# An attention and gated-linear-attention block on one core: the attention units' instructions in the order of the source, their weights loaded from ScalarE's queue, and a unit's first two weight groups taken tile by tile

## The chip, the cores and the metric

The kernel runs on one core of a Trainium2 chip. A core has five engines with a queue of instructions each: TensorE (PE in the profile, with its weight loads as PEld), VectorE (DVE), ScalarE (ACT), GpSimd (POOL) and SyncE (SP), which here only issues transfers. The metric is the device time of one execution in microseconds.

## The reference

One encoder block on a sequence of 512 tokens of width 2048, all float32:

```python
mod = silu(c) @ w_cond + b_cond                     # shift, scale, gate
h = rms_norm(x) * (1 + scale) + shift
proj = h @ w_in                                     # 2048 x 7200
aq, ak, av, ag, gq, gk, gv, gg, lr_f, lr_b = split(proj)
# 16 heads x 64: three dilated windows, merged by their softmax denominators, shared bias by distance
a_out = dilated_attention(aq, ak, av, rel_bias) * silu(ag)
# 4 heads, dk 128, dv 256: gated linear attention, forward and backward, decay from lr_f and lr_b
g_out = rms_norm(gla_fwd + gla_bwd) * gain * silu(gg)
y = concat(a_out, g_out) @ w_out
out = rms_norm(x + gate * y) * final_gain
```

## The kernel before

Every large product is made of three matmuls (`three`): each operand is split into a high part, rounded to the type that TensorE takes in one pass, and a low part, the remainder, and high x high, high x low and low x high are summed. A weight group is 128 x 1024 numbers (0.5 MB). `fetch` loads it into one of four `raw` buffers, `split_hi` makes the high part on ScalarE and `split_lo` the low part on DVE (a split); there are three buffers for high parts and three for low parts.

After a start that computes shift and scale, the values and the first queries and keys, the work is a row of **units**: qk2, qk4, qk6, gk, gv0, gv1, ag0, ag1, gg0, gg1, o0 to o3. A unit multiplies eight weight groups with the 512 tokens into four accumulators (tiles) of 128 x 512 in PSUM. For each group it goes over the four tiles, with two steps (ticks) of three matmuls for each, so a unit has 64 ticks and 192 projection matmuls. While it runs a group it splits the next and fetches those behind. There are five PSUM buffers for accumulators, tagged `pj`, and three for everything else, tagged `pa`. In the names of the rows, ps_qk_0 is the first accumulator of such a unit, qk40h the high part of unit qk4's group 0, and qk41l the low part of its group 1.

Between the ticks a unit does **side work**, a list of pairs (place in the unit from 0 to 1, step). In qk2, qk4, qk6 and gk it is the attention of four heads each, 16 tiles of scores of 128 queries x 512 keys. One tile's steps:

- `score`: two matmuls; DVE adds the bias tile `g` of the head and finds the row's minimum; ScalarE takes the exponential with the row sums; DVE takes the reciprocal and GpSimd scales the rows
- `turn`: four transposes on TensorE; ScalarE copies the result (high part), DVE subtracts it (low part)
- `values`, for two tiles at once: eight matmuls; ScalarE copies one half and DVE adds it to the other

A place of 1 or more moves a step into the next unit. When a unit of queries and keys ends, `qk_evict` takes its four accumulators apart, two for each pair of heads: for each accumulator ScalarE copies one half for one head, DVE the remainder, and again for the other head, and SyncE copies halves between partitions. These are the queries and keys of the next unit's attention.

`sum_work` is a list of 48 weighted sums on DVE over 0.5 MB each, loaded into the same `raw` buffers: 16 for a bias of the values and 32 for the gate. `SUMS_IN` says how many of them each unit takes as side work.

The **order of the work** is set in two ways. TensorE's instructions stand in the order of the source. On the other engines the first part has an order that a planner computes; from `qk_evict` on, a list scheduler places each instruction by priority and by when its operands are expected, and side work has a raised priority (`urgent`). SyncE issues nearly all transfers.

Of the kernel before, what the change touches and what calls it, by code (L numbers as in the profile page):

```python
# [72 lines left out]
ATT_AT = (0.17, 0.8, 0.04, 0.05, 0.05)  # L73
# [4 lines left out]
SUMS_IN = {"qk6": 4, "gk": 4, "gv0": 9, "gv1": 2, "ag0": 7, "ag1": 9, "gg0": 9}  # L78
# [55 lines left out]
def block_kernel(ctx: ExitStack, tc: tile.TileContext, a: dict):  # L134
# [421 lines left out]
    def attention(pairs):  # L556

        tiles = [(2 * p + j, i) for p in pairs for j in range(2) for i in range(4)]
        gt, pt, pr_ = {}, {}, {}
        heads = [2 * p + j for p in pairs for j in range(2)]  # L560

        def g_load(h):
            g = gp.tile([P, 896], F32, tag="g", name=f"g{h}")
            nc.sync.dma_start(g, bass.AP(grow.tensor, grow.offset + h * 1024, [[1, P], [1, 896]]))
            gt[h] = g

        def score(h, i):
            def go():
                if h % 8 == 0 and i == 0:
                    cat[h // 8] = B8(f"cat{h // 8}", [4, 512])  # L570
# [12 lines left out]
                act(t, t, AF.Exp, bias=st[:, 0:1], scale=-1.0, accum_out=st[:, 1:2])  # L583
                nc.vector.reciprocal(st[:, 2:3], st[:, 1:2])  # L584
# [4 lines left out]
        def turn(h, i):  # L589
            def go():  # L590
# [7 lines left out]
                hi = pt[h, half][:, 0, :, P * ii:P * ii + P]  # L598
                lo = pt[h, half][:, 1, :, P * ii:P * ii + P]
# [4 lines left out]

        def values(h, half):
            def go():
                t = pt.pop((h, half))
# [25 lines left out]
        at[0] -= move0  # L633
        at[1] -= move1
        at[-1] += move_last
        return list(zip(at, items))
# [206 lines left out]
    def unit(name, natural, side=(), rhs=None, lr=None, tiles=range(4)):  # L843
# [287 lines left out]
```

## Time and profile before

| | |
|---|---|
| runs | 958.15, 958.9 and 960.98 us, median 958.9 |
| the profiled execution | 959.9 us, its span 957.9 us |
| busy: PE, PEld, DVE, ACT, POOL | 939.7, 777.1, 605.3, 431.5, 81.1 us |
| granted clock of TensorE | 0.997 of full, as a mean |
| read from memory | 154.51 MB, 166 GB/s over the span |
| qk2, qk4, qk6, gk | 191.9 to 257.3, to 323.7, to 390.3, to 457.5 us |
| gv0 | 457.5 to 510.4 us |

Matmuls are pipelined, so a matmul's row lasts longer (0.39 us) than the distance to the next one (0.23 us); the chain of waits shows the distance. A row of the timeline gives its start, its length, the engine and line, what is written and read, and in brackets the idle time before it and what ended that. Buffer numbers are left out of names in the profile.

### The profile page before, as it was taken

What the parts mean: (1) busy time and instruction counts of PE and PEld (TensorE: products, weight loads), DVE (VectorE), ACT (ScalarE), POOL (GpSimd) and SP (SyncE); (2) the same over time, 40 slices, a digit from 0 to 9 for tenths busy, and PEclk for the clock granted to TensorE, in tenths of its full rate; (3) what the DMA queues carried; (4) which work ended last, traced back from release to release, by engine and by line L of the source; (5) the groups of instructions that cost most, each with busy time, mean ns of one, the idle gap of its engine ahead of it and who ended that gap; (6) DMA issues with size and microseconds to landing.
All of it is one profiled execution on the core that took longest, in us unless ns stands there. A gap on an engine that the chain in (4) does not pass through costs nothing.

```text
span 957.9 us, 11999 instructions
## 1 busy us (share of the span) xinstructions
PE 939.7 (98%) x4464; PEld 777.1 (81%) x4464; DVE 605.3 (63%) x900; ACT 431.5 (45%) x719; POOL 81.1 (8%) x100
## 2 busy tenths in 40 slices
PE   8999999999999999999999999999999999999996
PEld 5888788888888888888778888888887888888884
DVE  7988899675756676766435656675964352546421
ACT  5443533565655655655215544543834152233222
POOL 0000000012122022122000000000010000202120
PEclk9999999999999999999999999999999999999998
DMA  9999687443333463533454244354555464244013
GB/s 330 413 411 365 229 296 275 150 131 105 112 103 105 144 200 108 173 127 103 150 176 146 86 132 154 132 176 154 173 195 183 132 221 154 92 151 152 23 55 121
DMA packets 45180, 163.76 MB, mean 171 GB/s; under 512 B 5730, under 2 KB 6018, under 8 KB 40386
## 3 DMA queue, kind: packets, MB, share of 16 engines
q1 hardware_dynamic: 44946, 162.68, 49.9%
q8 instruction: 35, 0.57, 0.2%
q10 hardware_dynamic: 176, 0.33, 0.1%
q14 instruction: 23, 0.18, 0.1%
HBM read 154.51 MB, written 4.28 MB: 166 GB/s over the span
## 4 chain that ended last, share of the span: by engine, by line
PE 84%; DMA 6%; DVE 5%; issue 3%; ACT 1%; SPq 0%; POOL 0%; ACTq 0%; DVEq 0%; POOLq 0%
PE ps_o L170 6%; PE ps_o L169 6%; PE ps_o L171 6%; DMA rawg<-in_wg 6%; PE ps_qk L170 5%; PE ps_qk L169 5%; PE ps_qk L171 5%; PE o L611 3%; PE sta L169 3%; PE sta L170 3%; PE sta L171 3%; PE stb L171 3%; PE stb L169 3%; PE stb L170 3%; PE ps_gv L171 3%; PE ps_gv L170 3%
## 5 line engine op out<-in xcount | busy, mean ns | idle before, releaser
L585 POOL TENSOR_SCALAR p<-p,st 128x512 f32<-128x512 f32 x64 | 45.5, 711 | 406.6 <-DVE st L584 357.9
L244 DVE CUSTOM_DVE_ANT_0 cb<-cb,sb,c_bcond 128x2048 f32<-128x2048 f32 (+1 forms) x32 | 73.4, 2294 | 0.0
L583 ACT ACTIVATE p<-p,st 128x512 f32<-128x512 f32 x64 | 46.1, 721 | 56.8 <-DVE st L580 56.3
L602 DVE TENSOR_TENSOR pt<-t,pt 128x512 fp32r<-128x512 f32 x64 | 44.0, 689 | 16.2 <-ACT pt L601 15.8
L580 DVE CUSTOM_DVE_ANT_0 p<-s,g 128x512 f32<-128x512 f32 x64 | 43.6, 687 | 14.8 <-PE s L577 14.5
L601 ACT ACTIVATE pt<-t 128x512 fp32r<-128x512 f32 x64 | 37.8, 592 | 10.2 <-PE t L597 9.2
L244 DVE CUSTOM_DVE_ANT_0 rawg<-rawg,sb,gate 128x1024 f32<-128x1024 f32 x16 | 20.5, 1283 | 29.6 <-DMA rawg<-in_wg 29.6
L611 PEld LDWEIGHTS o<-pt,vv 128*128 128x128 f32 x256 | 34.7, 188 | 5.0 <-DVE pt L602 2.2
L597 PEld LDWEIGHTS t<-c_ident,p 128*128 128x128 f32 x256 | 31.8, 140 | 8.5
L597 PE MATMUL t<-c_ident,p 128*128 128x128 f32 x256 | 38.3, 272 | 0.0
L611 PE MATMUL o<-pt,vv 128*128 128x256 f32 x256 | 36.6, 283 | 0.9 <-DVE pt L602 0.8
L244 DVE CUSTOM_DVE_ANT_0 rawg<-rawg,sb,c_bcond 128x1024 f32<-128x1024 f32 x16 | 20.5, 1283 | 26.3 <-DMA rawg<-in_wg 26.3
L1014 POOL TENSOR_TENSOR x<-x,fgain 128x512 f32<-128x512 f32 x12 | 20.3, 1696 | 185.3 <-ACT ysq L1012 185.3
L1012 ACT ACTIVATE ysq<-x 128x512 f32<-128x512 f32 x16 | 10.1, 632 | 47.2 <-DVE x L1010 47.2
L767 POOL TENSOR_SCALAR dc<-st,sc 128x256 f32<-128x256 f32 x16 | 10.4, 652 | 245.5 <-DVE st L764 240.6
L1009 DVE TENSOR_TENSOR y<-ps_o,sb 128x512 f32<-128x512 f32 x16 | 10.9, 684 | 25.9 <-PE ps_o L171 25.9
L584 DVE RECIPROCAL st<-st 128x1 f32<-128x1 f32 x64 | 10.3, 162 | 24.9 <-ACT p L583 24.9
L576 PE MATMUL s<-ks,qs 128*128 128x512 f32 x64 | 25.1, 391 | 0.0
L577 PE MATMUL s<-kl,qs 128*128 128x512 f32 x64 | 25.0, 391 | 0.0
L774 ACT ACTIVATE sq<-st,sc 128x256 f32<-128x256 f32 x24 | 12.2, 509 | 26.8 <-DVE st L769 14.3
L1010 DVE TENSOR_TENSOR x<-y,x 128x512 f32<-128x512 f32 x16 | 18.0, 1125 | 0.3
L614 ACT ACTIVATE oh<-o 64x256 f32<-64x256 f32 x32 | 12.2, 382 | 13.0 <-PE o L611 12.2
(1275 smaller groups left out, 2916.7 us busy)
## 6 DMA issues: line engine op xcount, KB each, us to landing
cb<-in_wm SPq DMA_DIRECT2D x31, 1024.0 KB, 7.9
rawg<-in_wg SPq DMA_DIRECT2D x32, 512.0 KB, 3.4
raw_o<-in_w_o SPq DMA_DIRECT2D x32, 512.0 KB, 3.4
raw_qk<-in_w_qk SPq DMA_DIRECT2D x24, 512.0 KB, 3.4
rawb<-in_w_sb SPq DMA_DIRECT2D x16, 512.0 KB, 4.8
rawv<-in_wv SPq DMA_DIRECT2D x16, 512.0 KB, 3.8
raw_gv<-in_w_gv SPq DMA_DIRECT2D x16, 512.0 KB, 3.5
raw_ag<-in_w_ag SPq DMA_DIRECT2D x16, 512.0 KB, 3.3
```

The source lines that it names most:

```text
L169: mm(ps, lh, rh, start=first, stop=False)
L170: mm(ps, ll, rh, start=False, stop=False)
L171: mm(ps, lh, rl, start=False, stop=last)
L244: nc.vector.tensor_tensor_reduce(out=w, in0=w, in1=with_, op0=ALU.mult, op1=ALU.add, scale=1.0, scalar=init, accum_out=dst)
L576: mm(ps, qs[:, q], ks, start=True, stop=False)
L580: nc.vector.tensor_tensor_reduce(out=t, in0=ps, in1=gt[h][:, P * i:P * i + 512], op0=ALU.add, op1=ALU.min, scale=1.0, scalar=3e38, accum_o ...
L583: act(t, t, AF.Exp, bias=st[:, 0:1], scale=-1.0, accum_out=st[:, 1:2])
L585: nc.gpsimd.tensor_scalar(t, t, st[:, 2:3], 1.0, op0=ALU.mult, op1=ALU.mult)
L597: nc.tensor.transpose(pk[:, kt * P:kt * P + P], t[:, kt * P:kt * P + P], ident)
L601: act(hi, src, AF.Copy)
L602: tt(lo, src, hi.bitcast(F32), op=ALU.subtract)
L611: mm(po[:, :256], vv[h // 4][:, kt, h % 4, :], t[:, w, kt, :], start=kt == 0 and w == 0, stop=kt == 3 and w == 1)
```

## The change

It does five things. (1) From the first `qk_evict` to the end of gv0's matmuls, `tc.manual_schedule(engines=PLANNED)` gives DVE, ScalarE, GpSimd and SyncE the order of the source too. (2) The places of the attention's steps are new: a tile's score stands at 0.12 + 0.057 x of the unit (x from 0 to 15), its scaling 0.75 steps later, its turn 1.8 and its values 2.9 steps later; the last tiles' steps fall into the next unit. Scaling is a step of its own. (3) The weight groups of qk2, qk4, qk6 and gk and the bias tiles `g` are loaded from ScalarE's queue. (4) In these four units the first two groups are one step: each tile is taken through both before the next tile begins, and both have to be split. (5) The sums leave qk6 and gk; gv0 gets 12 (9 before), gv1 5 (2), ag0 8 (7), and gg1 the remaining 5 (4). The low-rank gate weights `lrs` are loaded and split in gk instead of behind it. The diff also brings another way of turning tiles, through memory (`turn`, `leave`, `back` and two more), which an empty `BY_DVE` leaves unused; it is left out here.

```diff
-ATT_AT = (0.17, 0.8, 0.04, 0.05, 0.05)
+ATT_AT = (0.12, 0.057)
+BY_DVE = ()
...
-SUMS_IN = {"qk6": 4, "gk": 4, "gv0": 9, "gv1": 2, "ag0": 7, "ag1": 9, "gg0": 9}
+SUMS_IN = {"gv0": 12, "gv1": 5, "ag0": 8, "ag1": 9, "gg0": 9}
...
             raws[i] = RAW(f"raw_{u}{g}", [2, 512])
-            nc.sync.dma_start(raws[i], a["w_" + u][g])
+            queue = nc.scalar if u[:2] in ("qk", "gk") else nc.sync
+            queue.dma_start(raws[i], a["w_" + u][g])
...
-            nc.sync.dma_start(g, bass.AP(grow.tensor, grow.offset + h * 1024, [[1, P], [1, 896]]))
+            nc.scalar.dma_start(g, bass.AP(grow.tensor, grow.offset + h * 1024, [[1, P], [1, 896]]))
...
                 act(t, t, AF.Exp, bias=st[:, 0:1], scale=-1.0, accum_out=st[:, 1:2])
+                pr_[h, i] = t, st
+            return go
+
+        def scale(h, i):
+
+            def go():
+                t, st = pr_.pop((h, i))
                 nc.vector.reciprocal(st[:, 2:3], st[:, 1:2])
                 nc.gpsimd.tensor_scalar(t, t, st[:, 2:3], 1.0, op0=ALU.mult, op1=ALU.mult)
                 pr_[h, i] = t
             return go
...
-        for x in range(n + 4):
-            if x < n:
-                items.append(score(*tiles[x]))
-            if 2 <= x <= n + 1:
-                items.append(turn(*tiles[x - 2]))
-            if 3 <= x <= n + 2 and tiles[x - 3][1] % 2 == 1:
-                items.append(values(tiles[x - 3][0], tiles[x - 3][1] // 2))
+        for x in range(n):
+            h, i = tiles[x]
+            items.append((x, score(h, i)))
+            items.append((x + 0.75, scale(h, i)))
...
+                items.append((x + 1.8, pe_turn(h, i)))
+                if ii:
+                    items.append((x + 2.9, values(h, half)))
+        items.sort(key=lambda v: v[0])
         g_load(heads[0])
-        start, span, move0, move1, move_last = ATT_AT
-        at = [start + (q + 0.5) / len(items) * span for q in range(len(items))]
...
+        start, step = ATT_AT
+        return [(start + step * x, go) for x, go in items]
...
-        for q in range(KT // 2):
-            g = gorder[q] if name == "o3" else q
-            i0 = gi[name, g]
+        order_ = gorder if name == "o3" else list(range(KT // 2))
+
+        steps = [order_[:2]] if name[:2] in ("qk", "gk") else [order_[:1], order_[1:2]]
+        for step in steps + [[g] for g in order_[2:]]:
             todo = []
             if 0 in tiles:
-                todo = list(range(gi[name, gorder[0] if name == "o3" else 0], upto[name, g] + 1))
+                todo = list(range(gi[name, order_[0]], upto[name, step[-1]] + 1))
                 for i in todo:
                     split_hi(i)
                 for ahead in (1, 2):
-                    fetch(upto[name, g] + ahead)
-            if i0 not in low:
-                split_lo(i0)
-            hi, lo = wts[i0]
+                    fetch(upto[name, step[-1]] + ahead)
+            for g in step:
+                split_lo(gi[name, g])
             for n, i in enumerate(tiles):
-                for kk in range(2):
...
+                for g in step:
+                    hi, lo = wts[gi[name, g]]
+                    for kk in range(2):
...
-    for p in range(2):
-        qk_evict(p, psb["b", 4 + 2 * p], psb["b", 5 + 2 * p])
-    for n, p in (("qk2", 0), ("qk4", 2), ("qk6", 4)):
-        ps = unit(n, False, attention((p, p + 1)) + ([(0.05, shift_row)] + some_sums(n) if p == 4 else []))
...
+    with tc.manual_schedule(engines=PLANNED):
+        for p in range(2):
+            qk_evict(p, psb["b", 4 + 2 * p], psb["b", 5 + 2 * p])
+        for n, p in (("qk2", 0), ("qk4", 2), ("qk6", 4)):
+            ps = unit(n, False, attention((p, p + 1)) + ([(0.6, shift_row)] if p == 4 else []))
+            for q in range(2):
+                qk_evict(p + 2 + q, ps[2 * q], ps[2 * q + 1])
...
+        ps = unit("gk", False, attention((6, 7)) + [(0.7, lr_load), (0.85, lambda: lr_part(0)), (0.9, lambda: lr_part(1))])
...
+        ps = unit("gv0", True, some_sums("gv0"), lr=lr_tick)
```

How this moves instructions shows in the order in which they stand on an engine. First ScalarE at the boundary from qk2 to qk4, before (p is a tile's exponential, pt the copy of a turn, oh that of a values step, qs and ks the evicted halves of queries and keys):

```order
L313 ACTIVATE qk41h<-raw_qk_1961 128x1024
L583 ACTIVATE p_2036,st_2037<-p_2036,st_2037 128x512
L601 ACTIVATE pt_2004<-t_2050 128x4x128
L539 ACTIVATE qs_2106<-ps_qk_0_1509 64x512
L601 ACTIVATE pt_2061<-t_2062 128x4x128
L539 ACTIVATE qs_2109<-ps_qk_0_1509 64x512
L614 ACTIVATE oh_2081<-o_2072 64x256
L548 ACTIVATE ks_2112<-ps_qk_1_1510 64x512
L601 ACTIVATE pt_2061<-t_2090 128x4x128
L548 ACTIVATE ks_2118<-ps_qk_1_1510 64x512
L539 ACTIVATE qs_2124<-ps_qk_2_1511 64x512
L313 ACTIVATE qk42h<-raw_qk_2045 128x1024
```

And the same place on ScalarE after the change:

```order
L586 ACTIVATE p_2072,st_2073<-p_2072,st_2073 128x512
L544 ACTIVATE qs_2079<-ps_qk_0_1511 64x512
L544 ACTIVATE qs_2082<-ps_qk_0_1511 64x512
L553 ACTIVATE ks_2085<-ps_qk_1_1512 64x512
L553 ACTIVATE ks_2091<-ps_qk_1_1512 64x512
L544 ACTIVATE qs_2097<-ps_qk_2_1513 64x512
L544 ACTIVATE qs_2100<-ps_qk_2_1513 64x512
L553 ACTIVATE ks_2103<-ps_qk_3_1514 64x512
L553 ACTIVATE ks_2109<-ps_qk_3_1514 64x512
L569 DMA g_2115<-grow 128x896
L318 ACTIVATE qk41h<-raw_qk_1932 128x1024
L318 ACTIVATE qk42h<-raw_qk_2007 128x1024
```

The high part of qk4's second group stood ahead of the last exponential and of all evictions; now it stands behind the last exponential, the eight evictions and the issue of a bias tile.

TensorE at the same boundary, before, from the last matmul of qk2 on:

```order
L171 MATMUL ps_qk_3_1512<-h_lo,qk27h 128x512
L169 MATMUL ps_qk_0_2144<-h_hi,qk40h 128x512
L170 MATMUL ps_qk_0_2144<-h_hi,qk40l 128x512
L171 MATMUL ps_qk_0_2144<-h_lo,qk40h 128x512
L611 MATMUL o_2156<-pt_2061,vv_921 128x256 x8
L169 MATMUL ps_qk_0_2144<-h_hi,qk40h 128x512
L170 MATMUL ps_qk_0_2144<-h_hi,qk40l 128x512
L171 MATMUL ps_qk_0_2144<-h_lo,qk40h 128x512
L169 MATMUL ps_qk_1_2145<-h_hi,qk40h 128x512
```

And TensorE after the change, from the last tile's score on (s is a score, t a turn, o a values step):

```order
L580 MATMUL s_2069<-kl_1504,qs_1494 128x512
L173 MATMUL ps_qk_3_1514<-h_hi,qk27h 128x512
L174 MATMUL ps_qk_3_1514<-h_hi,qk27l 128x512
L175 MATMUL ps_qk_3_1514<-h_lo,qk27h 128x512
L173 MATMUL ps_qk_0_2117<-h_hi,qk40h 128x512
L174 MATMUL ps_qk_0_2117<-h_hi,qk40l 128x512
L175 MATMUL ps_qk_0_2117<-h_lo,qk40h 128x512
L173 MATMUL ps_qk_0_2117<-h_hi,qk40h 128x512
L174 MATMUL ps_qk_0_2117<-h_hi,qk40l 128x512
L175 MATMUL ps_qk_0_2117<-h_lo,qk40h 128x512
```

Right behind these rows stand the turn and the values step that the unit before left over, and then the second group's first matmul:

```order
L608 MATMUL t_2142<-c_ident,p_2044 128x128 x4
L665 MATMUL o_2149<-pt_2021,vv_921 128x256 x8
L173 MATMUL ps_qk_0_2117<-h_hi,qk41h 128x512
L174 MATMUL ps_qk_0_2117<-h_hi,qk41l 128x512
L175 MATMUL ps_qk_0_2117<-h_lo,qk41h 128x512
```

Before, the second accumulator came next with the first group; now the first accumulator goes on with the second group, after six projection matmuls of the unit.

DVE at the start of qk2, before, from a remainder (kl) of the first pair's keys on (ISA rows are a tile's reduction):

```order
L550 TENSOR_TENSOR kl_1478<-stb_882,ks_1477 64x512
L297 TENSOR_TENSOR qk22l<-raw_qk_1513,qk22h 128x1024
L550 TENSOR_TENSOR kl_1484<-stb_882,ks_1483 64x512
L540 SCALAR_TENSOR_TENSOR qs_1489<-stb_887,qs_1489 64x512
L540 SCALAR_TENSOR_TENSOR qs_1492<-stb_887,qs_1492 64x512
L550 TENSOR_TENSOR kl_1496<-stb_894,ks_1495 64x512
L297 TENSOR_TENSOR qk23l<-raw_qk_1515,qk23h 128x1024
L550 TENSOR_TENSOR kl_1502<-stb_894,ks_1501 64x512
L580 ISA p_1553,st_1554<-s_1550,g_1507 128x512
```

And after:

```order
L555 TENSOR_TENSOR kl_1480<-stb_882,ks_1479 64x512
L555 TENSOR_TENSOR kl_1486<-stb_882,ks_1485 64x512
L545 SCALAR_TENSOR_TENSOR qs_1491<-stb_887,qs_1491 64x512
L545 SCALAR_TENSOR_TENSOR qs_1494<-stb_887,qs_1494 64x512
L555 TENSOR_TENSOR kl_1498<-stb_894,ks_1497 64x512
L555 TENSOR_TENSOR kl_1504<-stb_894,ks_1503 64x512
L302 TENSOR_TENSOR qk22l<-raw_qk_1515,qk22h 128x1024
L583 ISA p_1552,st_1553<-s_1549,g_1509 128x512
```

The low part of the third group stood between the evictions; now it stands behind them, directly ahead of the first tile's reduction. On ScalarE the issue of that group's load stands behind the evictions too.

More of the change, by code (lines that the diff above doesn't have):

```diff
@@ L597, in go @@
                     nc.tensor.transpose(pk[:, kt * P:kt * P + P], t[:, kt * P:kt * P + P], ident)
-                hi = pt[h, half][:, 0, :, P * ii:P * ii + P]
-                lo = pt[h, half][:, 1, :, P * ii:P * ii + P]
+                hi, lo = [pt[h, half][:, e, :, P * ii:P * ii + P] for e in range(2)]
                 src = pk.rearrange("p (k q) -> p k q", k=4)
@@ new lines, in unit @@
+                for g in step:
+                    hi, lo = wts[gi[name, g]]
+                    for kk in range(2):
+                        k = 2 * g + kk
+                        rh, rl = (h_hi[:, k, :], h_lo[:, k, :]) if rhs is None else rhs[k]
+                        first, last = (g, kk) == (order_[0], 0), (g, kk) == (order_[-1], 1)
+                        if natural:
+                            t = slice(i * P, i * P + P)
+                            cw = slice(kk * 512, kk * 512 + 512)
+                            three(ps[n], rh[:, t], rl[:, t], hi[:, cw], lo[:, cw], first, last)
+                        else:
+                            c = slice(kk * 512 + i * P, kk * 512 + i * P + P)
+                            three(ps[n], hi[:, c], lo[:, c], rh, rl, first, last)
+                        tick += 1
+                        if tick % (2 * len(tiles)) == 2:
+                            for i_ in todo:
+                                split_lo(i_)
+                        while pos < len(side) and side[pos][0] * ticks <= tick:
+                            urgent(side[pos][1])
+                            pos += 1
+                    if lr is not None:
+                        lr(4 * g + i)
```

111 lines of the change are left out of this document (66 added, 45 removed).

## The prediction

> **What bounds the kernel now.** I read the page's head first, then the table of stages, then what TensorE waits for.
>
> ```profile
> span 957.9 us, 11999 instructions
> PE 939.7 (98%) x4464; PEld 777.1 (81%) x4464; DVE 605.3 (63%) x900; ACT 431.5 (45%) x719; POOL 81.1 (8%) x100
> ```
>
> TensorE is busy in 98% of the span. Other engines matter only where they make it wait. The next rows are the stages: start and end, then busy time of PE, PEld, DVE, ACT and POOL, the granted clock, DMA. They are the four units that carry attention (qk2, qk4, qk6, gk) and gv0.
>
> ```profile
> 191.90:257.30 65.40, 65.37 (x346) 54.89 (x345) 43.50 (x90) 38.81 (x75) 11.15 (x16) 1.00 0.37 113
> 257.30:323.70 66.40, 66.37 (x353) 55.90 (x352) 41.93 (x89) 37.43 (x72) 11.17 (x16) 1.00 0.36 108
> 323.70:390.30 66.60, 66.57 (x355) 55.89 (x354) 47.24 (x100) 37.60 (x73) 11.13 (x16) 1.00 0.51 162
> 390.30:457.50 67.20, 66.36 (x353) 55.91 (x352) 44.98 (x94) 36.50 (x70) 12.05 (x16) 1.00 0.42 132
> 457.50:510.40 52.90, 52.52 (x234) 41.21 (x233) 20.16 (x26) 12.16 (x15) 0.00 (x0) 1.00 0.46 150
> ```
>
> TensorE has no gap in the first three units, 0.8 us in gk and 0.4 us in gv0. DVE and ACT have a third of each unit free. TensorE's own waits say what those gaps are:
>
> ```profile
> PE gn L819 <- ACT gsh L817: 1.2, 1, 1.2
> PE go L805 <- DVE at L791: 1.0, 1, 1.0
> PE o L611 <- DVE pt L602: 0.8, 1, 0.8
> PE plr L924 <- DVE lrs L917: 0.4, 1, 0.4
> ```
>
> Only the last two lie in the changed units, so all that a better order there can give back is 0.8 + 0.4 = 1.2 us. The question is what the written order costs. I time it with these rows: TensorE's steps from the chain of waits, the steps of a tile of scores from the timeline.
>
> ```profile
> 204.27 0.44 PE t L597 x4
> 204.71 0.23 PE ps_qk L169
> 204.94 0.23 PE ps_qk L170
> ...
> 210.68 0.94 PE o L611 x8
> ```
>
> ```profile
> 257.49 1.06 ACT L313 ACTIVATE qk42h<-raw_qk 128x1024 fp32r<-128x1024 f32 x1 [0.25 <-PE ps_qk L171]
> 258.58 1.23 DVE L297 TENSOR_TENSOR qk42l<-raw_qk,qk42h 128x1024 fp32r<-128x1024 f32 x1 [0.42 <-ACT qk42h L313]
> ...
> 266.26 0.69 DVE L580 CUSTOM_DVE_ANT_0 p<-s,g 128x512 f32<-128x512 f32 x1
> 267.00 0.72 ACT L583 ACTIVATE p<-p,st 128x512 f32<-128x512 f32 x1 [2.02 <-DVE st L580]
> 267.72 0.71 ACT L583 ACTIVATE p<-p,st 128x512 f32<-128x512 f32 x1
> 267.84 0.16 DVE L584 RECIPROCAL st<-st 128x1 f32<-128x1 f32 x1 [0.27 <-ACT p L583]
> 268.17 1.40 POOL L585 TENSOR_SCALAR p<-p,st 128x512 f32<-128x512 f32 x2 [15.91 <-DVE st L584]
> 269.60 0.39 PE L577 MATMUL s<-kl,qs 128*128 128x512 f32 x1
> 270.14 0.69 DVE L580 CUSTOM_DVE_ANT_0 p<-s,g 128x512 f32<-128x512 f32 x1 [1.43 <-PE s L577]
> ```
>
> A projection matmul takes 0.23 us of TensorE, a turn (four transposes) 0.44, a values step 0.94. From a score's second matmul to DVE's reduction is 0.54 us (269.60 to 270.14), from there to ScalarE's exponential 0.74, ScalarE is free 0.72 later; from exponential to reciprocal 0.84, to GpSimd's scaling 0.33, and that takes 0.70. A split into high and low part starts DVE 1.09 us after ScalarE and takes it 1.23.
>
> **The unit boundary (qk2 to qk4, qk4 to qk6, qk6 to gk): the large term.** When a unit ends, its four accumulators are evicted, and the next unit needs its second weight group split.
>
> ```profile
> 250.10 1.22 DVE L297 TENSOR_TENSOR qk41l<-raw_qk,qk41h 128x1024 fp32r<-128x1024 f32 x1
> ```
>
> Today that split is done at 251.3, 6 us before qk4 begins at 257.3. In the new order it stands behind all eight evictions on both engines, and these stand behind the last tile's exponential. At the same time the tile-by-tile start asks for the second group after only 6 projection matmuls instead of 24. How long eviction takes shows at the start of qk2, where little else runs (ScalarE, then a DVE row):
>
> ```profile
> 187.59 2.35 ACT L439 ACTIVATE gqt<-stb 128x512 f32<-128x512 f32 x4
> 190.02 0.59 ACT L539 ACTIVATE qs<-stb 64x512 fp32r<-64x512 f32 x1
> ...
> 191.99 0.59 ACT L548 ACTIVATE ks<-stb 64x512 fp32r<-64x512 f32 x1
> ...
> 194.17 0.59 ACT L539 ACTIVATE qs<-stb 64x512 fp32r<-64x512 f32 x1
> ```
>
> ```profile
> 190.65 0.68 DVE L540 SCALAR_TENSOR_TENSOR qs<-stb,qs 64x512 fp32r<-64x512 f32 x1 [1.71 <-ACT qs L539]
> ```
>
> The two engines take turns on an accumulator, so one pair (four of the eight) takes ScalarE 194.17 - 190.02 = 4.15 us, and two pairs 8.3. ScalarE then also issues the load of a bias tile. The one issue from its queue in the trace:
>
> ```profile
> 15.55 0.36 ACTq L259 DMA_DIRECT2D grow<-first  x1
> ```
>
> Count from the new unit's first matmul as zero. The last tile's second score matmul starts four matmuls earlier, at -0.92. Reduction -0.38, exponential +0.36, ScalarE free +1.08, evictions done 9.4, load issued 9.74, DVE's split begins 10.83 and ends 12.06. TensorE has by then run 6 projection matmuls (1.38), the turn and the values step left over from the unit before (0.44 + 0.94), and one matmul that needs only the high part (0.23): it is ready at 2.99. It waits 12.06 - 2.99 = **9.1 us**, three times, together **27.3 us**. Behind the waiting matmul stands all of TensorE's unit; the load queue is off the path, since loads were issued a group ahead. The next thing late is the last tile's turn, whose reciprocal stands behind a second split on DVE; it comes some 0.5 us late if TensorE is at full clock, and is covered if it is not.
>
> **The clock after such a wait.** At its start the kernel shows what a TensorE that has been idle does:
>
> ```profile
> 11.89 0.80 PE L169 MATMUL sta<-sa0h,h_hi 128*128 128x512 f32 x1
> ...
> 15.83 0.63 PE L171 MATMUL sta<-sa0l,h_hi 128*128 128x512 f32 x1
> 16.25 0.63 PE L169 MATMUL sta<-sa0h,h_hi 128*128 128x512 f32 x1
> ...
> 17.09 0.39 PE L171 MATMUL sta<-sa0l,h_hi 128*128 128x512 f32 x1
> 17.32 0.39 PE L169 MATMUL sta<-sa0h,h_hi 128*128 128x512 f32 x1
> ```
>
> Matmuls are 0.43 us apart until 17.09 and 0.23 after it: half speed for 17.09 - 11.89 = 5.2 us. And at its end: the last matmul, then two stages, where the number behind the five engines is the granted clock:
>
> ```profile
> 948.22 0.39 PE L171 MATMUL ps_o<-o36l,c_h 128*128 128x512 f32 x1
> ```
>
> ```profile
> 951.80:952.20 0.40, 0.00 (x0) 0.00 (x0) 0.37 (x1) 0.40 (x2) 0.40 (x1) 1.00 0.00 0
> 952.40:957.00 4.60, 0.00 (x0) 0.00 (x0) 0.00 (x0) 0.35 (x1) 0.33 (x1) 0.50 0.61 228
> ```
>
> The clock fell to half within 3.8 us of the last matmul's end (948.6). A wait of 9.1 us, broken by one matmul, is longer than that. So each boundary also pays 5.2 us at half speed, in which 1 - 0.23/0.43 = 0.47 of the time is lost: 2.4 us, three times **7.2 us**. Bounds: nothing, or 4.1 each if half speed is counted from the four matmuls at 8.3. The Trainium skill, "TensorE: Matmul & The Clock Gate", section "What's actually happening", states a full clock after about 3.4 us of sustained work; by that figure it would be 1.6 each and the sum below 2.4 us smaller. The start's 5.2 us speaks for the dearer price, though its first matmuls also had gaps.
>
> **The start of qk2.** Its first two groups are ready as today, but the third is now loaded by ScalarE, whose queue reaches the issue only after the evictions.
>
> ```profile
> raw_qk<-in_w_qk SPq DMA_DIRECT2D x24, 512.0 KB, 3.4
> ```
>
> Evictions 190.02 + 8.3 = 198.3, two issues 199.0 (the load goes out at about 198.7), landed 202.1, split done 1.09 + 1.23 later at 204.4. TensorE needs that only at its 17th step of three matmuls; but on DVE the first tile's reduction stands behind this split. So reduction 204.4, exponential 205.1, reciprocal 206.0, scaled 207.0. TensorE comes to the first turn after 45 projection and 4 score matmuls, 191.9 + 49 x 0.23 = 203.2. Wait: **3.8 us**. Bounds 2.5 (eviction a little faster) and 5.5 (slower landing, or the clock falls once more).
>
> **gk to gv0.** Here the evictions are four copies (2.35 us): ScalarE free 1.08, copies 3.43, split begun on DVE 4.52, done 5.75, then the last tile's reciprocal, scaled by 6.8. TensorE gets to that turn after 15 projection matmuls, a turn, a values step and two narrow matmuls: 5.3. Wait **1.5 us**; the 0.8 and 0.4 us of today go (**-1.2**).
>
> **Inside the units.** Score to turn takes 0.54 + 0.74 + 0.84 + 0.33 + 0.70 = 3.2 us, and TensorE gives it at least six steps of three matmuls, a turn and a score, some 5.2. Where a split comes between exponential and reciprocal (five of a unit's eight, by the written positions), it is 0.54 + 0.74 + 0.72 + 1.09 + 1.23 + 0.33 + 0.70 = 5.4, or 0.2 late on two or so of them: I take 0.4 per unit, **1.6 us**, between 0 and 8. Twelve loads per unit that move to ScalarE at 0.36 are 4 us of its free 28: nothing, as long as none waits. Eight sums leave the attention units and go to gv0, gv1, ag0 and gg1, where DVE has room (20 of 53 us in gv0): nothing, between -1 and +2.
>
> **The sum.** 27.3 + 7.2 + 3.8 + 1.5 - 1.2 + 1.6 = 40.2 us on the profiled execution's 959.9, so 1000.1. The median of the runs is 1.0 lower (958.9), so I forecast **999.1 us**.
>
> **Rivals.** (a) The clock holds over the wait: 33.0 us, 991.9. For it only that one matmul breaks the wait; against it the fall at the end. Chance 0.10. (b) The order costs inside the units too: a reduction that comes 0.7 us later behind the preceding tile's low part makes 0.9 us at each of 20 such splits, 18 instead of 1.6: 1015.5. Today's list order avoids just that; but most tiles have a values step more of cover. 0.10. (c) Evictions do not alternate, ScalarE runs its eight at 0.62: 5.0 instead of 8.3, waits of 5.8 and no clock loss, 17.4 + 3.8 + 1.5 - 1.2 + 1.6 = 23.1: 982.0. The gap between 190.02 and 191.99 for one accumulator speaks against it. 0.08. (d) Not slower: the second group's split ends before TensorE asks. It decides at 2.99 us after the unit's start; then only 1.2 us of waits go, 957.7. It would need ScalarE to reach it 9 us earlier, past an exponential whose score is computed four matmuls before the unit ends. 0.04.
>
> **How the numbers follow.** The forecast has 0.68. Its own ends: boundaries of 8.3 us (evictions 0.8 quicker) with a clock loss of 1.6 each, qk2 at 2.5 and nothing inside the units, 29.7 + 2.5 + 1.5 - 1.2 = 32.5 or 991.4; and a clock loss of 4.1 each, qk2 at 5.5 and 8 us inside the units, 27.3 + 12.3 + 5.5 + 1.5 - 1.2 + 8 = 53.4 or 1012.3. The range 988 to 1012 holds it and (a), and leaves out (c), (d) and most of (b), 0.2 in all. A measurement here tells 0.3% (2.9 us) from no change; no case gains that, so faster has 0.01, same 0.03, slower 0.96.
>
> **What would show it.** Right: in the new trace TensorE waits once some 2 to 3 us into qk4, qk6 and gk for the low part of the second group, about 9 us, with eight evictions in a row on ScalarE before; matmuls 0.43 us apart after it; one wait of about 4 us at the first turn of qk2. Wrong: those waits under 5 us, a clock of 1.00 across them, or as much waiting spread over the turns inside the units.

## The result, and the profile after

The changed kernel takes 1001.33 us (median of 4 runs, 998.12 to 1003.59) against 959.0 us for the one before beside it (4 runs, 958.15 to 960.98): a ratio of 1.0436, 95% interval 1.0397 to 1.0475. The profiled execution took 1003.59 us, its span 1001.6, 43.7 more than before.

The head of the page of the changed kernel, busy times by engine:

```profile
span 1001.6 us, 11901 instructions
PE 951.2 (95%) x4464; PEld 784.6 (78%) x4464; DVE 603.5 (60%) x901; ACT 430.8 (43%) x720; POOL 78.9 (8%) x100
```

No engine has more to do: VectorE and ScalarE are busy as long as before. TensorE has the same matmuls; its 11.5 us more come with a mean granted clock of 0.976 against 0.997, and the rest of the 43.7 us is idle time. The table of stages of the changed kernel, for qk2, qk4, qk6, gk, gv0 and gv1 (start and end, busy time of PE, PEld, DVE, ACT and POOL, granted clock, DMA):

```profile
192.70:265.70 73.00, 66.10 (x330) 55.04 (x329) 36.90 (x80) 32.88 (x64) 10.41 (x15) 0.93 0.35 105
265.70:342.50 76.80, 68.81 (x353) 57.19 (x352) 41.04 (x89) 37.30 (x72) 11.09 (x16) 0.93 0.32 93
342.50:420.30 77.80, 69.81 (x355) 57.93 (x354) 41.17 (x89) 37.52 (x73) 11.11 (x16) 0.93 0.35 105
420.30:496.70 76.40, 68.42 (x354) 56.94 (x353) 41.17 (x90) 37.91 (x74) 11.11 (x16) 0.96 0.38 111
496.70:552.40 55.70, 54.33 (x250) 42.93 (x248) 28.35 (x41) 16.10 (x23) 0.69 (x1) 1.00 0.60 198
552.40:610.60 58.20, 56.02 (x271) 46.96 (x270) 37.30 (x50) 26.77 (x47) 1.91 (x4) 0.97 0.45 146
```

Against before, qk2 is 7.6 us longer, qk4 10.4, qk6 11.2, gk 9.2, gv0 2.8 and gv1 4.0. (qk2 also has fewer instructions: two turns and a values step, by the prediction's prices about 1.8 us, are pushed on from unit to unit and arrive in gv0.) gg0 is 2.4 us shorter (54.2 against 56.6 us). This execution is the slowest of the four runs, 2.3 us above their median. TensorE's own waits name the places:

```profile
PE t L608 <- POOL p L595: 8.3, 2, 6.9
PE ps_qk L173 <- ACT qk61h L318: 7.5, 1, 7.5
PE ps_qk L173 <- ACT qk41h L318: 7.5, 1, 7.5
PE ps_gk L173 <- ACT gk1h L318: 7.5, 1, 7.5
PE kt L804 <- DVE ki L794: 2.2, 1, 2.2
PE ps_qk L174 <- DVE qk41l L302: 0.5, 1, 0.5
```

At each of three boundaries TensorE waits for the second group, first for its high part and then for its low part; 6.9 us at one turn, which is qk2's first; 2.2 us in gv1. The boundary of qk2 to qk4 in the timeline of the changed kernel:

```profile
265.65 0.39 PE L173 MATMUL ps_qk<-h_hi,qk40h 128*128 128x512 f32 x1
...
266.00 0.72 ACT L586 ACTIVATE p<-p,st 128x512 f32<-128x512 f32 x1 [1.41 <-DVE st L583]
266.72 0.57 ACT L544 ACTIVATE qs<-ps_qk 64x512 fp32r<-64x512 f32 x1
268.05 0.59 ACT L544 ACTIVATE qs<-ps_qk 64x512 fp32r<-64x512 f32 x1 [0.75 <-DVE qs L545]
...
274.37 0.59 ACT L553 ACTIVATE ks<-ps_qk 64x512 fp32r<-64x512 f32 x1 [0.92 <-DVE kl L555]
274.45 0.35 ACTq L569 DMA_DIRECT2D g<-grow  x1
274.98 1.06 ACT L318 ACTIVATE qk41h<-raw_qk 128x1024 fp32r<-128x1024 f32 x1
276.07 1.23 DVE L302 TENSOR_TENSOR qk41l<-raw_qk,qk41h 128x1024 fp32r<-128x1024 f32 x1 [0.39 <-ACT qk41h L318]
276.09 0.80 PE L173 MATMUL ps_qk<-h_hi,qk41h 128*128 128x512 f32 x1 [7.53 <-ACT qk41h L318]
277.35 0.80 PE L174 MATMUL ps_qk<-h_hi,qk41l 128*128 128x512 f32 x1 [0.46 <-DVE qk41l L302]
```

The unit starts at 265.65. ScalarE does the last tile's exponential, then eight evictions in a row from 266.72 to 274.96, each second one waiting for VectorE's half of the same accumulator, and only then the split that TensorE has been asking for since it finished the few steps that it had. Two stages around the wait, in the same columns as above:

```profile
265.60:271.00 5.40, 2.97 (x19) 2.43 (x18) 2.69 (x6) 3.34 (x7) 0.00 (x0) 1.00 0.10 22
271.00:281.20 10.20, 4.65 (x11) 3.27 (x12) 6.73 (x10) 5.07 (x8) 0.69 (x1) 0.50 0.82 189
```

The clock is at half from 271.0, in the wait, to 281.2. TensorE works from 277.35 on, so it runs 3.9 us at half speed.

### The profile page after: what moved, and what is told of

It reads as the page before. It is cut to its first block, busy times and chain, and to the rows that moved or that the text cites. A ratio compares the mean times of both kernels' runs of the same rounds, so it can differ in the third digit from the quotient of the medians.

```text
span 1001.6 us, 11901 instructions
## 1 busy us (share of the span) xinstructions
PE 951.2 (95%) x4464; PEld 784.6 (78%) x4464; DVE 603.5 (60%) x901; ACT 430.8 (43%) x720; POOL 78.9 (8%) x100
## 5 line engine op out<-in xcount | busy, mean ns | idle before, releaser
L612 DVE TENSOR_TENSOR pt<-t,pt 128x512 fp32r<-128x512 f32 x64 | 43.9, 687 | 40.2 <-ACT pt L611 40.1
L583 DVE CUSTOM_DVE_ANT_0 p<-s,g 128x512 f32<-128x512 f32 x64 | 43.8, 685 | 11.4 <-PE s L580 10.4
L611 ACT ACTIVATE pt<-t 128x512 fp32r<-128x512 f32 x64 | 37.9, 592 | 26.7 <-PE t L608 25.9
L608 PEld LDWEIGHTS t<-c_ident,p 128*128 128x128 f32 x256 | 32.1, 144 | 18.8 <-POOL p L595 11.2
L672 DVE TENSOR_TENSOR cat<-o,oh 64x256 f32<-64x256 f32 x32 | 13.2, 413 | 10.1 <-ACT oh L668 9.5
```

The costliest lines, as they stand in the source:

```text
L583: nc.vector.tensor_tensor_reduce(out=t, in0=ps, in1=gt[h][:, P * i:P * i + 512], op0=ALU.add, op1=ALU.min, scale=1.0, scalar=3e38, accum_o ...
L608: nc.tensor.transpose(pk[:, kt * P:kt * P + P], t[:, kt * P:kt * P + P], ident)
L611: act(hi, src, AF.Copy)
L612: tt(lo, src, hi.bitcast(F32), op=ALU.subtract)
```

## The experiments

The theory is the prediction's: a written order that puts the block of evictions ahead of the second group's split. Its rivals: the queue, the tile by tile groups, or a fixed order as such. All ratios are against the kernel before, run on the same chip; the changed kernel's own ratio is 1.0436. The kernel before took 957.6 to 958.1 us beside the experiments and 959.0 beside the changed kernel, whose four runs lie 5.5 us apart. So differences of medians against the changed kernel carry an uncertainty of some 2 us (by the ratios they are up to 2 us smaller), and where less is at stake single units are compared.

**The list scheduler again, all else as changed.**

```diff
-    with tc.manual_schedule(engines=PLANNED):
+    with ExitStack():
         for p in range(2):
             qk_evict(p, psb["b", 4 + 2 * p], psb["b", 5 + 2 * p])
```

> Undoes one of the three parts: the second stage's instructions are put in order by the list scheduler again on all five engines; ScalarE's queue for the weights, the tile by tile first groups and the moved sums stay. Theory (the written order holds the second group's split behind the evictions): the 8.7 us wait at the start of qk4, qk6 and gk goes, its half clock after it and qk2's 7.1 us too, 3 x (8.7 + 1.9) + 9 = about 41 us, so some 960 us, no stretch at half clock between the first matmuls and the end. Rival (ScalarE's queue or the tile by tile loads are the cause, whatever the order): the waits stay within 2 us of today's and the time stays at 995 to 1003 us.

Measured: 974.68 us, ratio 1.0178 (1.0155 to 1.0202). 26.7 us come back, not 41. The 7.5 us waits and the 6.9 us one are gone. TensorE's longest waits in this kernel are others:

```profile
PE s L580 <- DMA kl<-kl: 6.5, 3, 2.3
PE s L579 <- DMA ks<-ks: 6.3, 4, 2.3
```

They are the first scores of the four units, which wait for the copies of the keys between partitions (12.8 us in all), with a stretch of 3.4 to 3.6 us at half clock in each of the four units. So the theory was right about the waits it names, and wrong that nothing else costs. That the copies land late shows in the issues of this kernel, with the median time to landing at the end of a row, and then in those of the kernel before:

```profile
ks<-ks SPq DMA_DIRECT2D x16, 128.0 KB, 5.1
kl<-kl SPq DMA_DIRECT2D x16, 128.0 KB, 4.3
```

```profile
ks<-ks SPq DMA_DIRECT2D x16, 128.0 KB, 2.2
kl<-kl SPq DMA_DIRECT2D x16, 128.0 KB, 2.4
```

**The second group's split alone moved ahead, written order kept.**

```diff
                 todo = list(range(gi[name, order_[0]], upto[name, step[-1]] + 1))
+                after_ = {"qk2": "qk4", "qk4": "qk6", "qk6": "gk"}.get(name)
+                if after_ and step[-1] == KT // 2 - 1:
+                    todo.append(gi[after_, 1])
```

> The written order stays; only the second group's split of qk4, qk6 and gk is written into the last step of the unit before, ahead of the evictions. Rival theory (the late split alone is the trouble): TensorE runs on at the start of those units, 3 x (8.7 + 1.9) = 32 us less, about 970 us. Theory (the whole block of eight evictions is the trouble, on VectorE too): the split is in time, but the last tile's reciprocal on VectorE stands behind the same evictions and the third group's split, is ready about 13 us after the unit starts, and TensorE, which asks for the scaled tile at about 5 us, waits some 8 us there: 0 to 1.5 us less per boundary, 997 to 1001 us, the three half clock stretches kept.

Measured: 1000.44 us, ratio 1.0444 (1.0424 to 1.0463): nothing gained. The timeline of this kernel at the same boundary (qk4 starts at 263.6):

```profile
274.65 1.23 DVE L302 TENSOR_TENSOR qk42l<-raw_qk,qk42h 128x1024 fp32r<-128x1024 f32 x1 [0.39 <-ACT qk42h L318]
275.80 0.15 DVE L594 RECIPROCAL st<-st 128x1 f32<-128x1 f32 x1
276.12 0.69 POOL L595 TENSOR_SCALAR p<-p,st 128x512 f32<-128x512 f32 x1 [12.48 <-DVE st L594]
276.87 1.11 PE L608 MATMUL t<-c_ident,p 128*128 128x128 f32 x4 [7.89 <-POOL p L595]
```

The wait, 7.9 us, is nearly as long and has only moved: the last tile's exponential was done at 265.4, but its reciprocal stands behind VectorE's eight halves of the evictions and the third group's split, and starts at 275.8. It is the block as a whole that costs, on both engines.

**The wait filled with unused matmuls.**

```diff
+                    if n == 0 and g == 1 and name in ("qk4", "qk6", "gk"):
+                        warm = PA("warm")
+                        for z in range(30):
+                            mm(warm, wts[gi[name, 0]][0][:, :P], h_hi[:, 0, :], start=True, stop=True)
                     hi, lo = wts[gi[name, g]]
```

> Adds 30 matmuls of 128x512 into an unused accumulator, not read by anything, ahead of the second group in the first step of qk4, qk6 and gk: 30 x 0.23 = 6.9 us of work inside the 8.7 us wait. Theory (the half clock after the wait is a second price, beside the wait): the wait's end does not move, the granted clock stays at 1.00 through the three boundaries, and 1.8 + 2.6 + 1.4 = 5.8 us are saved, about 995.5 us. Rival (the half clock costs nothing of its own since later turns absorb it): no change within 1 us, 1001 us.

Measured: 996.0 us, ratio 1.0397 (1.0382 to 1.0413), 5.3 us less. The stage around the same boundary in this kernel (qk4 from 264.4):

```profile
270.00:280.00 10.00, 8.54 (x38) 6.31 (x37) 6.99 (x11) 5.49 (x9) 0.69 (x1) 1.00 0.83 203
```

The clock stays at 1.00, at all three boundaries and behind them. The three units are 1.6, 2.3 and 1.2 us shorter, 5.1 in all: that is the price of the half clock by itself.

**qk2's third group fetched ahead of the evictions.**

```diff
+        fetch(2)
         for p in range(2):
             qk_evict(p, psb["b", 4 + 2 * p], psb["b", 5 + 2 * p])
```

> One statement moved: ScalarE issues the load of qk2's third group before the first evictions, not behind them; all else as in the changed kernel. Theory (qk2's first turn waits for that load, which landed 7.1 us after its issue): the load lands by 200 us, the split of the third group is done a few us after the evictions, the 7.1 us wait at qk2's first turn shrinks to under 1 us and the half clock after it (2.6 us) goes: 7 to 9.5 us less, 992 to 994 us. Rival (the wait is the evictions' on VectorE, the load only ends last by a little): 0 to 3 us less.

Measured: 994.31 us, ratio 1.0379 (1.0357 to 1.0401), 7.0 us less; qk2 is 7.2 us shorter, 65.8 long. Its first turn still waits 2.2 us, for another load:

```profile
202.71 0.69 DVE L583 CUSTOM_DVE_ANT_0 p<-s,g 128x512 f32<-128x512 f32 x1 [2.21 <-DMA g<-grow]
```

The first reduction needs the head's bias tile, whose load ScalarE also issues only behind the evictions.

**SyncE's queue again, in the written order, and then with the list scheduler.**

```diff
-            queue = nc.scalar if u[:2] in ("qk", "gk") else nc.sync
+            queue = nc.sync
...
-            nc.scalar.dma_start(g, bass.AP(grow.tensor, grow.offset + h * 1024, [[1, P], [1, 896]]))
+            nc.sync.dma_start(g, bass.AP(grow.tensor, grow.offset + h * 1024, [[1, P], [1, 896]]))
```

> Undoes one part alone: the weights of qk2, qk4, qk6 and gk and the bias tiles are loaded from SyncE's queue again, in the written order of the changed kernel. Theory (under the written order the block of evictions sets the boundary, whichever queue loads): the 8.7 us waits stay, 998 to 1003 us; the third group's load of qk2 now stands behind the eviction's copies on SyncE, which wait for the same evictions, so qk2's wait of 7 us stays too. Rival (ScalarE's queue is what costs): 980 us or less.

> The kernel with the list scheduler (974.7 us) and the loads of the attention units on SyncE's queue again; the tile by tile first groups, the places of the attention's steps and the moved sums stay. Theory (what the list order left, waits of TensorE for ks and kl of 1.7 to 2.5 us each, is the price of ScalarE's queue: its loads ran beside the copies of ks and kl, which landed in 4.3 to 5.1 us against 2.3): the copies land in about 2.3 us again, the waits and the 2 us at half clock after them go, 3 x 5 + 2 = 17 us less, 957 to 960 us. Rival (the tile by tile groups put off the evictions and with them the first scores): waits and time stay, 972 to 976 us.

Measured: 1000.33 us, ratio 1.0432 (1.0407 to 1.0457), in the written order, with the 7.5 us waits of the changed kernel and 7.2 us at qk2's first turn, as the theory had it; 958.65 us, ratio 1.0008 (0.9995 to 1.0021), with the list scheduler. The issues and TensorE's wait for the copies in the latter:

```profile
ks<-ks SPq DMA_DIRECT2D x16, 128.0 KB, 2.5
kl<-kl SPq DMA_DIRECT2D x16, 128.0 KB, 2.3
```

```profile
PE s L579 <- DMA ks<-ks: 2.2, 2, 1.5
```

The two parts are not additive. With the list scheduler ScalarE's queue costs 974.68 - 958.65 = 16.0 us: between the two profiled executions TensorE waits 10.6 us less for the copies, and four stretches at half clock, some 1.6 us each, are gone. In the written order the queue costs 1001.33 - 1000.33 = 1.0, which the spread of the runs covers. The issues of the changed kernel show why; its copies are not late as a rule:

```profile
ks<-ks SPq DMA_DIRECT2D x16, 128.0 KB, 2.2
kl<-kl SPq DMA_DIRECT2D x16, 128.0 KB, 2.3
```

There the loads are issued behind the evictions (274.45 and 274.89 at the boundary shown above). Copies issued ahead of them land in 2.2 us, those issued beside them, for the second pair, in 4.8 to 5.8 (medians by boundary; single copies take up to 7.8), but no score waits for one. The list scheduler with ScalarE's queue put the loads among the copies. From its timeline at the same boundary, where qk4 begins at 260.41:

```profile
263.45 0.33 ACTq L569 DMA_DIRECT2D g<-grow  x1
263.69 0.46 SPq L554 DMA_DIRECT2D ks<-ks  x1
264.48 0.34 ACTq L291 DMA_DIRECT2D raw_qk<-in_w_qk  x1
```

With SyncE's queue it issued the same two loads 0.3 and 2.6 us into the unit, instead of 3.0 and 4.1, and the first copy at 3.3 us as here. Even so the first pair's copies at that boundary landed in 5.4 us (ks) and 4.9 (kl), behind a load on their own queue, and the second pair's in 2.6 and 2.3. So a copy is late when bulk loads are in flight with it, on either queue; what the queue changes here is when the loads are issued. Loads on ScalarE's queue at SyncE's times were not run.

With SyncE's queue the written order costs 1000.33 - 958.65 = 41.7 us. And everything else that the change does (tile by tile groups, places, sums, earlier `lrs`) gives together no difference that can be measured.

**The first two groups one after the other again**, as in the kernel before (list scheduler, SyncE's queue):

```diff
-        steps = [order_[:2]] if name[:2] in ("qk", "gk") else [order_[:1], order_[1:2]]
+        steps = [order_[:1], order_[1:2]]
```

> As the one before it, and the first two groups one after the other again, not tile by tile: what is left of the change are the places of the attention's steps, the moved sums and the earlier load of the low-rank weights. If the tile by tile step costs or gains nothing of its own: within 2 us of the kernel with the list scheduler and SyncE's queue. If it is what puts off the evictions: 5 to 15 us less than that kernel. If it gives the evictions the time they need: 3 to 10 us more.

Measured: 963.54 us, ratio 1.0055 (1.0036 to 1.0074), 4.9 us more than with the tile by tile groups. At each of the three boundaries TensorE waits twice, 0.8 and 0.5 us, for accumulators not yet evicted. So tile by tile gains about what the other three parts (places, sums, earlier `lrs`) lose together: it asks for the next free accumulator later.

**ScalarE's queue alone, in the kernel before.**

```diff
-            nc.sync.dma_start(raws[i], a["w_" + u][g])
+            queue = nc.scalar if u[:2] in ("qk", "gk") else nc.sync
+            queue.dma_start(raws[i], a["w_" + u][g])
```

and the same for `g`.

> The kernel before with one part of the change alone: the weights of the attention units and the bias tiles g are loaded from ScalarE's queue; the list scheduler, the places, the groups and the sums are those of before. Theory (on a queue of their own the loads run beside the copies of ks and kl, which stand in front of the first scores): the copies land in 4 to 5 us against 2.3, the first scores, which come 6.9 us into the unit, wait 1 to 5 us at three boundaries: 961 to 973 us. Rival (the collision needs the tile by tile groups, which fetch two groups at once there): 956 to 960 us.

Measured: 960.28 us, ratio 1.0027 (1.0016 to 1.0039), 2.6 us more, between the theory's range and the rival's, 0.3 above the latter. The copies land in 3.1 (ks) and 3.3 us (kl), and TensorE waits 1.1 us for one of them, in qk2, the only attention unit that got much longer (1.7 us). The delay is there without the tile by tile groups, but smaller, and mostly hidden. The price of the queue depends on what its loads meet; 16 us was this combination's.

**The written order repaired.**

```diff
+EVICT_AT = (0.019, 0.045, 0.085, 0.15)
+SPLIT_AT = 0.17
...
+            side = sorted(side + list(zip(EVICT_AT, evict)) +
+                          [(SPLIT_AT, lambda i=i: split(i)) for i in first_step] +
+                          [(SPLIT_AT, lambda i=upto[name, 1] + ahead: fetch(i)) for ahead in (1, 2)],
+                          key=lambda x: x[0])
```

with the second group's split ahead and `fetch(2)` as above; `evict` holds the four accumulators' evictions of the unit before.

> The written order is kept and repaired: the second group is split in the unit before, qk2's third group is loaded ahead of the evictions, and the evictions of the four accumulators stand as side work at places 0.019, 0.045, 0.085 and 0.15 of the next unit, behind the last tile's reciprocal, with the third group's split and two loads moved behind them to 0.17. Theory (not the written order as such but the block of eight evictions ahead of everything costs): the 8.7 us waits and the half clock after them go, 3 x 10.6 + 7.2 = 39 us less, 962 us; 961 to 972 us if first scores wait a few us for the copies. Rival (a fixed order on VectorE and ScalarE costs in itself): waits of 5 us and more appear at turns and accumulators in these units, 985 us or more.

Measured: 975.58 us, ratio 1.018 (1.016 to 1.0201): 25.8 us back, fewer than the theory's 29 to 40, more than the rival allows. The 7.5 us waits at the boundaries and the half clock behind them are gone; one stretch of 3.6 us at half clock is left, in qk2, behind a wait of 2.3 us. What is left at turns is eight smaller waits:

```profile
PE t L607 <- POOL p L594: 9.8, 8, 2.3
```

The timeline behind one of them:

```profile
275.33 1.73 POOL L594 TENSOR_SCALAR p<-p,st 128x512 f32<-128x512 f32 x1 [12.65 <-ACT qk42h L320]
275.33 1.25 DVE L304 TENSOR_TENSOR qk42l<-raw_qk,qk42h 128x1024 fp32r<-128x1024 f32 x1 [0.20 <-ACT qk42h L320]
277.11 0.66 PE L607 MATMUL t<-c_ident,p 128*128 128x128 f32 x4 [1.80 <-POOL p L594]
```

So most of the price was the block of evictions. This kernel loads from ScalarE's queue, and the list scheduler with that queue takes 974.68 us (ratio 1.0178 against 1.018): repaired, the written order costs no more than the list order with that queue. Both are 16 to 17 us above the list order with SyncE's queue (2 to 4.5 us in each of the four units for the repaired one), but with different waits: here turns wait for GpSimd, and the copies land in 2.2 and 2.4 us; there scores wait for copies. The repaired order with SyncE's queue, or with other places, was not tried.

**Fewer sums in gv1** (2 for 5, and 8 in gg1), changed kernel otherwise:

```diff
-SUMS_IN = {"gv0": 12, "gv1": 5, "ag0": 8, "ag1": 9, "gg0": 9}
+SUMS_IN = {"gv0": 12, "gv1": 2, "ag0": 8, "ag1": 9, "gg0": 9}
```

> The changed kernel with 2 sums in gv1, as before the change, instead of 5, and 8 in gg1 instead of 5. Theory (gv1 is 4.0 us longer since its first head's chain on VectorE stands behind sums that wait for their loads, so the second direction's gates come 2.3 us late): TensorE's wait for ki in gv1 goes, gv1 takes 54.2 to 55 us again, 3 to 4 us less in all, 997 to 998.5 us. Rival (gv1's wait comes from the steps that gv0 pushes on, not from the sums): gv1 stays within 1 us of 58 us.

Measured: 999.85 us, ratio 1.0435 (1.0417 to 1.0453), 1.5 us less by the medians and nothing by the ratios, less than the theory's 3 to 4; so the unit has to answer. gv1 in the table of stages of this kernel:

```profile
553.00:607.20 54.20, 54.20 (x271) 45.89 (x271) 33.80 (x44) 26.94 (x47) 1.91 (x4) 1.00 0.39 127
```

54.2 us as before the change, 4.0 less than in the changed kernel, and no wait for `ki`. The 4.0 us are one execution's: in the four experiments above that keep the written order and 5 sums in gv1 (split ahead, unused matmuls, early fetch, SyncE's queue) the unit takes 55.1 to 56.0 us, with waits for `ki` of 0.7 to 1.6 us and no half clock. So the sums are the cause, at 1 to 2 us as a rule and 4 where the clock falls as well, which fits the small difference of the medians.

**Later first scores and fewer sums in four units**: list scheduler, SyncE's queue, tile by tile groups, and

```diff
-ATT_AT = (0.12, 0.057)
+ATT_AT = (0.15, 0.055)
...
-SUMS_IN = {"gv0": 12, "gv1": 5, "ag0": 8, "ag1": 9, "gg0": 9}
+SUMS_IN = {"gv0": 12, "gv1": 2, "ag0": 7, "ag1": 7, "gg0": 7}
```

> From the kernel with the list scheduler, SyncE's queue and the tile by tile groups (958.65 us): the first score of an attention unit at place 0.15 with steps of 0.055 (0.12 and 0.057 before), and fewer sums in gv1, ag0, ag1 and gg0 (2, 7, 7, 7), 13 in gg1. Theory (what is left there are the first scores' waits for ks of 1.7 and 0.8 us and the waits of gv1 and ag1 of 1.4 and 1.5 us for chains on VectorE that stand among the sums): these go, 5 us less and some 1.5 us of gg0's, 952 to 955 us. Rival (later scores push more steps into the next unit, where they put off the evictions by as much): the waits come back, 957 to 960 us.

Measured: 954.0 us (6 runs, 953.3 to 954.36), ratio 0.9957 (0.9945 to 0.9969): 0.4% less than the kernel before, a small difference but clear of its interval. TensorE has four waits over 0.1 us left in this kernel, the longest 3.3 us, and all of them lie in the start.

Later first scores give the copies their time, and gg1, where VectorE was busy for 26 of 53 us, takes the sums. The two edits were not run apart; against the kernel that this one starts from, the four attention units are 3.4 us shorter, and the stretch from gv0 to gg0, which holds the units with fewer sums, 4.1.

## Why the prediction was right, and where not

The forecast was 999.1 us, the measurement 1001.33, inside the range; the mechanism is the forecast's own. Term by term, in the profiled executions (the terms' sum was 40.2; the spans differ by 43.7, and the changed kernel's profiled run is 2.3 us above its median):

- **Boundary wait, 27.3 us**: right, and the experiments bear the mechanism out. The split's low part is ready 277.3 - 265.65 = 11.7 us after the unit's start where the working had 12.06, and TensorE is held up 8.7 us (7.7 for the high part and 1.0 for the low part, start to start), three times, 26.1. ScalarE's issue of the bias tile cost nothing: it ran beside the last eviction (274.45 against 274.37 to 274.96), where the working added 0.36.
- **What is late next**: the working has the last tile's turn covered behind this wait. That holds, and the experiment with the split ahead shows the other half: were the split not late, that turn would wait 7.9 us instead.
- **Clock loss, 7.2 us**: the mechanism is right, the size is 5.1 (1.6, 2.3, 1.2), shown by the unused matmuls. The working took 5.2 us at half speed after each wait; it was 3.9, 5.5 and 2.9 us. The Trainium skill's 3.4 us ("TensorE: Matmul & The Clock Gate", "What's actually happening"), by the prediction's estimate 1.6 us per boundary and 4.8 in all, came nearer than the start's row; the stretches that the trace shows vary around it.
- **Start of qk2, 3.8 us**: the term that was mis-sized. The mechanism is right, but the wait is 7.1 us, and the clock fell as well (5.5 us at half speed after it, 0.47 of which is 2.6). qk2 is 7.6 us longer with some 1.8 us less work in it: 9.4 in place of 3.8, and beyond the working's own bound of 5.5, which has a slower landing or a fall of the clock, but not both at this size. The step that failed is "landed 202.1", 3.4 us after the issue by the median of such loads. The load here was the second of two, behind the 448 KB of a bias tile on its queue, with copies of ks and kl in flight beside both:

```profile
198.40 0.36 ACTq L569 DMA_DIRECT2D g<-grow  x1
198.80 0.51 ACTq L291 DMA_DIRECT2D raw_qk<-in_w_qk  x1
205.92 1.06 ACT L318 ACTIVATE qk22h<-raw_qk 128x1024 fp32r<-128x1024 f32 x1 [6.94 <-DMA raw_qk<-in_w_qk]
```

  ScalarE could split it 7.1 us after its issue. The load in this position at qk4's start took 7.6 us. How much of that is the bias tile and how much the copies was not separated. The early fetch took 7.2 us off the unit, as a wait for this load should.
- **gk to gv0, 1.5 us**: right, 1.55 at the turn. **Waits gone, -1.2**: 1.0 and 0.5, start to start.
- **Inside the units, 1.6 us**: nothing that shows; TensorE's waits list no other in these units. (The working's cover of some 5.2 us comes to 5.0 by its own rows, 18 matmuls, a turn and a score's two, so by them a turn would be 0.4 us late and not 0.2; none was.) Rival (b), which put the price there, did not come about.
- **Sums moved, 0**: wrong for gv1. The working looked at VectorE's free time in gv0 and not at gv1, where it gave 5 sums for 2. There a sum that waits for its load holds up the chain behind it on VectorE; the second direction's `ki` came 2.3 us late and a half clock followed, 4.0 us in all in this execution, 1 to 2 in others, which the run with fewer sums took away. gg0's 2.4 us less cancel part of it; why the waits of before there went is not settled, since the number of its sums is the same.
- **The sum as measured**: 26.1 + 5.1 + 9.4 + 1.5 - 1.5 + 4.0 - 2.4 = 42.2 us, and 0.8 ahead of qk2, which differs by as much between executions; 0.7 are not placed. That the forecast lies only 2.2 us off the median is in part luck: qk2 was 5.6 us too cheap and gv1 4.0, against 3.3 too much for boundaries and clock, 1.6 inside the units and gg0's 2.4.
- **Loads on ScalarE's queue, 0**: right for this kernel and only for it, since the list scheduler's kernel pays 16 us for the same loads. The prediction priced their issues and did not ask what else would be in flight with them: here the written order itself holds the loads back until the copies that are needed first have landed.

Rivals (a), (c) and (d) fell to single rows: the clock was 0.50 in the wait, the evictions alternate (266.72, 268.05), and the split was 8.7 us late.

## What to carry to other kernels

In a written order, find the longest run of instructions that nobody is waiting for, and see what stands behind it on each engine, since moving the one late instruction ahead only hands the wait to the next. A transfer's place in the order counts as much: small copies were late where a bulk load was in flight with them, and a change of queue moved the loads in time. A landing time taken from a median holds only for a transfer that meets what the median one meets. The price of one part can depend on another, so undo each part both with and without the other before calling one free.

## What the runs showed of the hardware

- How long TensorE stood still did not decide alone whether the clock fell. In gv1 of the changed kernel a wait of 2.18 us, behind steady work, was followed by 3.4 us at half; in the kernel with the early fetch a wait of the same length, also behind steady work, was not (the clock is 1.00 until 209):

```profile
580.74 0.55 PE L804 MATMUL kt<-c_ident,ki 128*128 128x128 f32 x3 [2.18 <-DVE ki L794]
581.60:585.00 3.40, 3.40 (x10) 2.64 (x9) 1.98 (x5) 1.23 (x3) 0.96 (x2) 0.50 0.77 253
```

```profile
205.30 0.66 PE L608 MATMUL t<-c_ident,p 128*128 128x128 f32 x4 [2.18 <-POOL p L595]
```

  Read in steps of 0.2 us, the stretches at half clock from qk2 to gv1 of these kernels lasted 3.4 to 3.6, 6.8 to 7.0 or 10.2 to 10.4 us, about one, two or three times the shortest. Part of a stretch lies in the wait, where it costs nothing: of the 10.2 us at the boundary shown above TensorE worked only through the last 3.9.

- A copy of 128 KB landed in 2.2 us when no bulk load was in flight with it, and in 4.8 to 5.8 us beside loads on another queue (changed kernel, boundaries) or in 5.4 and 4.9 behind one on its own queue (list scheduler, SyncE's queue). The Trainium skill ("Trainium Kernel Development and Optimization", "Key Constraints") says that transfers of different queues run on the same 16 DMA engines and interleave; this agrees.
- GpSimd's scaling took 1.73 us in the three places of the repaired order where it began together with VectorE's subtract of two operands that both lie in SBUF (1.25 us), 0.69 elsewhere. The Trainium skill ("SBUF — State Buffer", "SBUF: two separate sides") describes an exclusive lock between the two engines that would do this; the 1.04 us more are within the subtract's 1.25. That was not tested further. In each of the three places a turn waited 1.8 to 1.9 us for the scaling, so this is a part of what the repaired order still costs.
